# A hybrid decoder layer on one core: where its tiles start within 256 bytes of SBUF

## The chip, the cores and the metric

The kernel runs on one core of one Trainium2 chip. Its time is device microseconds for one launch. Before the change the median of three runs is 795.43 us (793.41 to 795.83).

## The reference

One layer on x of 512 tokens by 1024 features, all in float32:

```python
h = rms_norm(x, norm_mix_w)
z, xbc, dt, q, k, v, f = split(h @ w_in)                  # 1024 x 5664
x = x + concat([ssd(xbc, z, dt), fox(q, k, v, f)]) @ w_out  # 2048 x 1024
h = causal_conv3(rms_norm(x, norm_ffn_w) @ w_up)          # 1024 x 5632
gate, val = split(h)
x = x + (silu(gate) * val) @ w_down                       # 2816 x 1024
```

`ssd` is a chunked state-space mixer with 16 heads, `fox` is causal attention with 16 heads and a forget gate.

## The kernel before

**Products in three parts.** Every large product is made by `mm3` (line 101). A float32 operand A is split into a high part `ah` (rounded to the fp32r format) and a low part `al` = A - `ah`, and three matmuls are added into one PSUM bank: `ah*bh`, `ah*bl`, `al*bh`. ScalarE (ACT) rounds the high part with a copy, VectorE (DVE) makes the low part with a subtraction. Each matmul has a stationary operand of 128 columns, which PE loads ahead of it (the instruction LDWEIGHTS, shown as PEld), and a moving operand of 256 or 512 columns that is streamed through. In a matmul's name in the profile, `pw<-wh,xl` means: into the bank `pw`, moving `wh`, stationary `xl`.

**Three stages with different roles.** In the input projections, `feature_tile` (line 241) has weights stationary and the 512 tokens `xh`, `xl` moving; `wide_block` (line 346, banks `pw`) has tokens stationary and weights `wh`, `wl` moving; the output projection (`out_proj`, `out_part`, banks `po`) has the mixers' outputs stationary (`msh`, `msl` of the state-space heads, `mfh`, `mfl` of attention) and weights moving. All of these stream 512 columns. In the **up projection** weights are stationary and half the tokens are moving, so each matmul streams 256 columns. A Strassen-like scheme makes seven products of each of the inner "quads" of weight tiles (`n0` to `n6`, lines 906 to 969), each product of 24 matmuls; the first of the 11 quads is made plainly, as eight products of 24 (`plain`, line 1004). That is 10 x 168 + 192 = 1872 matmuls. Their moving operands are `uh`, `ul` (operands 0 to 3, in the buffers that `xh`, `xl` had), `sh`, `sl` (operands 4 to 6) and `ghl`. In the **down projection** (lines 1089 on) the gated products are stationary and weights move, 512 columns again, in seven products.

**Order.** All engines' programs are laid out ahead of time by a scheduler that works on the order of the code with priorities (`urgent`), and each engine then runs its list in order. The up projection takes 447 to 685 us of the profiled execution. In it a quad's weights arrive by DMA from SyncE's queue (SP), and three times a DMA of GpSimd's queue (POOL) adds another quarter to the same tile `Ta`; after each, ACT and DVE split it again. `gated` (line 982) makes the convolution on ACT and DVE and the gating on POOL.

**Kept products.** Three intermediate sums of a quad (`y0`, `z2`, `y3`) are copied from PSUM to SBUF by ACT (`keep`, line 896), into a ring of 4 buffers of 2 KB, and used once by DVE (lines 929, 965 and 959).

**Where tiles start.** SBUF addresses follow from the tiles' sizes and the order in which they are made. `small` (line 80) rounds small tiles up to `LINE` = 32 floats, 128 bytes. So every tile that PE reads starts either at 0 or at 128 modulo 256 (called its class here). A column slice that PE takes is a multiple of 256 bytes long, so the class of a tile holds for all slices. In the built program:

| tiles | class before | class after |
|---|---|---|
| `xh`, `xl`; `wh`, `wl` in `wp` (three of four pairs) | 128 | 128 |
| `wh`, `wl` in `pa` (every fourth pair) | 0 | 128 |
| `msh`, `msl`, `mfh`, `mfl` | 0 | 128 |
| `ident` (moving operand of the transposes) | 128 | 128 |
| what is transposed (`prob`, `tok`, `xs`, `y`, `xw`), and `qs`, `ks`, `sc`, `xdt`, `v`, `pt` | 0 | 128 |
| `uh`, `ul`, `sh`, `sl` (moving, up projection) | 128 | 64 |
| `ghl` (moving, 48 matmuls of the first quad) | 0 | 128 |
| the down projection's `oh`, `ol`, `oxh`, `oxl` | 128 | 128 |

"Offset" below is the class of a matmul's moving operand less the class of the stationary operand that PE loads for the next matmul while this one streams.

Of the kernel before, what the change touches and what calls it, by code (L numbers as in the profile page):

```python
# [8 lines left out]
F32 = mybir.dt.float32  # L9
F32R = mybir.dt.float32r  # L10
# [5 lines left out]
P = 128  # L16
SEQ = 512
D = 1024
NK = D // P
# [11 lines left out]
NFF = D_FF // P  # L31

AHEAD = 2000
LINE = 32
WARM = 8
C_SCW, C_SCB, C_FCW, C_FCB, C_QW, C_KW, C_END = 0, 48, 60, 192, 236, 237, 238

# [2 lines left out]
def tile_hybrid_layer(  # L40
# [23 lines left out]
    cp = ctx.enter_context(tc.tile_pool(name="cp", bufs=1))  # L64
# [15 lines left out]
    def small(pool_, shape, tag, bufs=1):  # L80

        n = 1
        for d in shape:
            n *= d
        t = pool_.tile([P, -(-n // LINE) * LINE], F32, tag=tag, name=tag, bufs=bufs)[:, 0:n]
        return t if len(shape) == 1 else t.rearrange("p (a b) -> p a b", b=shape[-1])
# [33 lines left out]
        pool.tensor_tensor(out=dst, in0=dst, in1=mhalf[:, 0 : shape], op=ALU.pow)  # L120

    pc = small(cp, (C_END,), "pc")
    misc = cp.tile([P, 2 * LINE], F32, tag="misc", name="misc")
    taken_columns = [0]

    def columns(n):
# [24 lines left out]
    pxt = ctx.enter_context(tc.tile_pool(name="pxt", bufs=1))  # L151
    actx = ExitStack()
    pa = actx.enter_context(tc.tile_pool(name="pa", bufs=1))
    xh = pxt.tile([P, NK, SEQ], F32R, tag="xh", name="xh")
    xl = pxt.tile([P, NK, SEQ], F32R, tag="xl", name="xl")
    R = pa.tile([P, SEQ], F32, tag="R", name="R")
    r = columns(NTB)
    rhalf = columns(NTB)
# [7 lines left out]
    first = [pa.tile([P, 1024], F32R, tag=t, name=t, bufs=1) for t in ("wh", "wl")]  # L166
# [577 lines left out]
    NH = NFF // 2  # L744
    HT = SEQ // 2
# [2 lines left out]

    ptt = ctx.enter_context(tc.tile_pool(name="ptt", bufs=1, side="right", reuse_waits="tile"))

    ptt.tile([P, 24], F32, tag="rest", name="rest", bufs=1)
    pu_ctx = ExitStack()
    pu = pu_ctx.enter_context(tc.tile_pool(name="pu", bufs=1, side="right", reuse_waits="tile"))
    up_banks = {"Z": pz}
# [2 lines left out]
        return up_banks[tag].tile([P, 2, 512], F32, tag=tag, name=name)  # L757


    oh = pxt.tile([P, NK, SEQ], F32R, tag="xh", name="uh").rearrange("p a b -> p (a b)")  # L760
    ol = pxt.tile([P, NK, SEQ], F32R, tag="xl", name="ul").rearrange("p a b -> p (a b)")
    oh, ol = [t.rearrange("p (n k t) -> p n k t", n=4, k=4) for t in (oh, ol)]
    sh, sl = [pu.tile([P, 3, 4, HT], F32R, tag=t, name=t) for t in ("sh", "sl")]

# [108 lines left out]
    def take(on_act, on_dve=None, at=None):  # L873
        taken[made[0] - 1 if at is None else at] = (on_act, on_dve)
# [19 lines left out]
                halfway[0] = ins  # L894

    def keep(src, name, at=None):
        t = pu.tile([P, 2, HT], F32, tag="kept", name=name, bufs=4)
        take(act.copy(t, src), at=at)
        return t

# [13 lines left out]
    def n0(q, where=None):  # L914
        u = quads[q]
        if not hasattr(u, "w"):
            n0_weights(q, where)
        u.G = two_banks("G", "G")
        product(u.w, 0, u.G, H2, True)
        with urgent():  # L920
            u.y0 = keep(u.G[:, :, H2], "y0", u.at)
# [9 lines left out]
    def n2(q):  # L931
        u = quads[q]
        w = split_up(u.ta)
        more(u.ta, B22, q)
        u.Z = two_banks("Z", "Z")
        product(w, 3, u.Z, H1, True)
        with urgent():
            u.z2 = keep(u.Z[:, :, H1], "z2")

    def n3(q):  # L940
        u = quads[q]
        w = split_up(u.ta)
        more(u.ta, B21, q)
        product(w, 4, u.G, H2)
        with urgent():
            u.y3 = keep(u.G[:, :, H2], "y3")
# [205 lines left out]
    pt_ = ctx.enter_context(tc.tile_pool(name="pt", bufs=1, side="right", reuse_waits="tile"))  # L1152
    held_ops = [pt_.tile([P, NH, HT], F32R, tag=t, name=t) for t in ("oh", "ol")]
    T += [pt_.tile([P, 512 * (b - a)], F32, tag="T%d" % a, name="T%d" % a) for a, b in UNITS[2:]]
    def operand(n):
        if n % 3 == 1:
            pair_ = [pxt.tile([P, NK, SEQ], F32R, tag=t, name="o" + t) for t in ("xh", "xl")]
            return tuple(
                t.rearrange("p a b -> p (a b)")[:, 0 : NH * HT].rearrange("p (a b) -> p a b", b=HT) for t in pair_
            )  # L1160
        if n == 2:
            return held_ops
        where = pt_ if n % 3 == 2 else pb
        return [where.tile([P, NH, HT], F32R, tag=t, name=t) for t in ("oh", "ol")]
# [24 lines left out]
    def units_of(n):  # L1189
        quarter, _, tiles, start, adds = PRODUCTS[n]  # L1190
        nxt = PRODUCTS[n + 1][1] if n + 1 < len(PRODUCTS) else None
        if nxt is not None:
            ops.append(operand(n + 1))
# [162 lines left out]
```

## Time and profile before

| | us |
|---|---|
| median of 3 runs | 795.43 |
| the profiled execution: its own time | 795.52 |
| its span, first to last instruction | 793.5 |
| PE busy | 779.5 (98%) |
| DVE busy | 617.6 (78%) |
| ACT busy | 476.7 (60%) |
| POOL busy | 252.3 (32%) |

The profiled execution is 0.09 us from the median, and 2.0 us of it lie outside the span. The granted clock of TensorE is full in it (0.998). A matmul's duration in the profile runs from its start to its modelled end and overlaps its successors: a matmul of 256 columns is shown with 283 ns though the next one starts 120 ns later. Since matmuls run in order, what PE needs for one is read from the distance between the starts of two, called the pitch here.

### The profile page before, as it was taken

How to read it: one execution, taken by the hardware profiler on the slowest of the kernel's cores; microseconds unless marked ns; L12 is line 12 of the kernel's file. 1: busy time of each engine (PE TensorE's matmuls, PEld its weight loads, DVE VectorE, ACT ScalarE, POOL GpSimd, SP SyncE). 2: the span in 40 equal slices, each digit the busy share in tenths (PEclk: the TensorE clock that was granted, in tenths of full speed). 3: DMA queues.
4: the chain of work that ended last, by engine and by line, in shares of the span. 5: the costliest groups of instructions: out<-in, count | busy, mean ns of one | idle time of the engine just before them, and what ended most of it. 6: DMA issues, size and time to landing. Idle time of an engine off the chain costs nothing.

```text
span 793.5 us, 12355 instructions
## 1 busy us (share of the span) xinstructions
PE 779.5 (98%) x4579; PEld 669.9 (84%) x4579; DVE 617.6 (78%) x923; ACT 476.7 (60%) x833; POOL 252.3 (32%) x296
## 2 busy tenths in 40 slices
PE   9999999999999999999999999999999999999996
PEld 7888877878887878887877999999999999888785
DVE  4896987688567576587875885997999998996674
ACT  7656546562479478685663664665656665765561
POOL 0004231443233362233200004444444443553120
PEclk9999999999999999999999999999999999999999
DMA  9514322431254144253222237788788877899992
GB/s 337 192 58 164 106 90 85 147 132 54 80 160 133 49 137 132 70 173 83 90 80 81 86 81 141 174 186 186 161 185 186 186 176 177 224 252 204 243 184 81
DMA packets 35723, 113.95 MB, mean 144 GB/s; under 512 B 4368, under 2 KB 5456, under 8 KB 35664
## 3 DMA queue, kind: packets, MB, share of 16 engines
q1 hardware_dynamic: 24896, 76.46, 28.3%
q0 software_dynamic: 10336, 36.18, 25.3%
q8 instruction: 36, 0.59, 0.3%
q10 hardware_dynamic: 432, 0.52, 0.2%
q14 instruction: 23, 0.19, 0.1%
HBM read 107.29 MB, written 2.20 MB: 138 GB/s over the span
## 4 chain that ended last, share of the span: by engine, by line
PE 67%; DVE 12%; DMA 8%; issue 7%; POOL 3%; ACT 3%; SPq 0%; POOLq 0%; DVEq 0%; ACTq 0%
PE pw L104 22%; PE po L104 11%; DVE wl L870 8%; PE g L104 6%; PE Z L104 6%; PE G L104 6%; DMA Ta<-in_wup_dram 3%; DVE ua L976 2%; PE o L634 2%; PE pT L624 2%; DMA T<-in_wdown_dram 2%; PE Y L104 2%; PE yd L460 2%; DMA Tb<-in_wup_dram 1%; PE j L104 1%
## 5 line engine op out<-in xcount | busy, mean ns | idle before, releaser
L104 PE MATMUL pw<-wh,xh 128*128 128x512 f32 x256 | 102.4, 402 | 0.0
L104 PE MATMUL pw<-wl,xh 128*128 128x512 f32 x256 | 101.8, 398 | 0.0
L104 PE MATMUL pw<-wh,xl 128*128 128x512 f32 x256 | 101.5, 398 | 0.0
L98 DVE TENSOR_TENSOR wl<-wraw,wh 128x1024 fp32r<-128x1024 f32 x59 | 76.0, 1288 | 15.1 <-ACT wh L97 14.7
L97 ACT CAST wh<-wraw 128x1024 fp32r<-128x1024 f32 x59 | 61.8, 1047 | 28.0 <-PE po L104 11.8
L104 PE MATMUL G<-uh,wh 128*128 128x256 f32 x264 | 75.0, 284 | 0.4 <-DVE Z L965 0.4
L104 PE MATMUL G<-uh,wl 128*128 128x256 f32 x264 | 74.7, 284 | 0.2 <-DVE wl L870 0.2
L104 PE MATMUL G<-ul,wh 128*128 128x256 f32 x264 | 74.7, 283 | 0.0
L870 ACT CAST wh<-Ta 128x1024 fp32r<-128x1024 f32 x40 | 41.9, 1048 | 36.5 <-DMA Ta<-in_wup_dram 24.5
L870 DVE TENSOR_TENSOR wl<-Ta,wh 128x1024 fp32r<-128x1024 f32 x40 | 50.2, 1261 | 8.7 <-ACT wh L870 8.7
L104 PEld LDWEIGHTS pw<-wh,xl 128*128 128x128 f32 x256 | 48.2, 188 | 10.0 <-issue 0.5
L104 PEld LDWEIGHTS pw<-wl,xh 128*128 128x128 f32 x256 | 48.2, 188 | 9.7 <-issue 0.7
L104 PEld LDWEIGHTS pw<-wh,xh 128*128 128x128 f32 x256 | 48.1, 188 | 9.6 <-issue 0.5
L870 DVE TENSOR_TENSOR wl<-Tb,wh 128x1024 fp32r<-128x1024 f32 x20 | 50.0, 2500 | 7.5 <-ACT wh L870 7.4
L904 POOL DMA_DIRECT2D Ta<-in_wup_dram x30 | 26.3, 877 | 81.8 <-DVE wl L870 81.5
L104 PEld LDWEIGHTS G<-uh,wh 128*128 128x128 f32 x264 | 50.6, 192 | 0.8 <-DVE Z L965 0.6
L104 PEld LDWEIGHTS G<-uh,wl 128*128 128x128 f32 x264 | 50.5, 192 | 0.5 <-DVE wl L870 0.5
L104 PEld LDWEIGHTS G<-ul,wh 128*128 128x128 f32 x264 | 50.6, 192 | 0.0
L1112 ACT CAST wh<-T 128x1024 fp32r<-128x1024 f32 (+1 forms) x30 | 29.4, 980 | 35.2 <-DMA T<-in_wdown_dram 16.7
L1112 DVE TENSOR_TENSOR wl<-T,wh 128x1024 fp32r<-128x1024 f32 (+1 forms) x30 | 34.0, 1134 | 20.5 <-ACT wh L1112 20.4
L603 DVE CUSTOM_DVE_ANT_0 prob<-S,prob 128x128 f32<-128x128 f32 (+1 forms) x64 | 30.3, 486 | 24.9 <-PE S L602 24.6
L607 ACT ACTIVATE prob<-prob,nm 128x128 f32<-128x128 f32 (+1 forms) x64 | 35.8, 560 | 21.1 <-DVE nm L603 20.8
(294 smaller groups left out, 2436.1 us busy)
## 6 DMA issues: line engine op xcount, KB each, us to landing
Ta<-in_wup_dram POOLq DMA_DIRECT2D x30, 512.0 KB, 5.5
T<-in_wdown_dram POOLq DMA_DIRECT2D x20, 512.0 KB, 7.8
wraw<-in_wqk_dram SPq DMA_DIRECT2D x16, 512.0 KB, 3.6
wraw<-in_wout_dram SPq DMA_DIRECT2D x16, 512.0 KB, 3.3
wraw<-in_wup_dram SPq DMA_DIRECT2D x14, 512.0 KB, 3.4
wraw<-in_wxbc_dram SPq DMA_DIRECT2D x11, 512.0 KB, 6.3
Ta<-in_wup_dram SPq DMA_DIRECT2D x10, 512.0 KB, 5.8
Tb<-in_wup_dram SPq DMA_DIRECT2D x10, 512.0 KB, 5.2
```

What stands on the lines that cost most here:

```text
L97: act.copy(h, r)
L98: dve.tensor_tensor(out=l, in0=r, in1=raw(h), op=ALU.subtract)
L104: ins = pe.matmul(o, a, b, start=start and n == 0, stop=stop and n == 2, **kw)
L460: pe.matmul(yd[:, h * HD : (h + 1) * HD], sc[:, h, :], xdt[:, h * HD : (h + 1) * HD], start=True, stop=True)
L603: dve.tensor_tensor_reduce(out=p, in0=sps[:, :n], in1=p, scale=-1.0, scalar=-NEG, op0=ALU.add, op1=ALU.min, accum_out=nm[:, qb : qb + 1],)
L607: act.activation(p, p, AF.Exp, scale=-1.0, bias=nm[:, qb : qb + 1], accum_out=sm[:, qb : qb + 1])
L624: pe.transpose(t[:, w : w + P], prob[:, o : o + P], ident)
L634: ins = pe.matmul(o[rows, kb * P :], v[:, kb, (2 * pair + i) % 8, :], pt[:, w : w + SEQ - kb * P], start=kb == 0, stop=kb == NTB - 1, skip ...
L870: ordered(act.copy(h, r), lambda: dve.tensor_tensor(out=l, in0=r, in1=raw(h), op=SUB))
L904: last_more[0] = nc.gpsimd.dma_start(t, wup[quarter, q], accum_op=ALU.add)
L976: dve.scalar_tensor_tensor(out=a[:, s:], in0=o[:, : SEQ - s], scalar=pc[:, cw + 2 - s : cw + 3 - s], in1=a[:, s:], op0=ALU.mult, op1=ALU.add,)
L1112: ordered(act.copy(hs, src[:, :n]), lambda: dve.tensor_tensor(out=ls, in0=src[:, :n], in1=raw(hs), op=SUB))
```

## The change

`LINE` becomes 64 floats, so `small` rounds to 256 bytes; `misc` keeps its 64 columns. The two big token tiles in the pool `pxt` are 256 bytes longer, and a helper `moved` gives a view into them that begins at a given float. `xh`, `xl` and the down projection's `oxh`, `oxl` begin at 0; `uh`, `ul` begin at float 48, which is 192 bytes on. A spacer tile ahead of the pool `pu` grows from 24 to 40 floats, so that `sh` and `sl` start 192 bytes past the class of the weights too, and another spacer of 48 floats stands in the pool `pt`. To make room the ring `kept` has 3 buffers in place of 4.

```diff
-LINE = 32
+LINE = 64
...
-    misc = cp.tile([P, 2 * LINE], F32, tag="misc", name="misc")
+    misc = cp.tile([P, LINE], F32, tag="misc", name="misc")
...
-    xh = pxt.tile([P, NK, SEQ], F32R, tag="xh", name="xh")
-    xl = pxt.tile([P, NK, SEQ], F32R, tag="xl", name="xl")
+
+    def moved(tag, name, first=0):
+        return pxt.tile([P, NK * SEQ + LINE], F32R, tag=tag, name=name)[:, first : first + NK * SEQ]
+
+    xh, xl = [moved(t, t).rearrange("p (a b) -> p a b", b=SEQ) for t in ("xh", "xl")]
...
-    ptt.tile([P, 24], F32, tag="rest", name="rest", bufs=1)
+    ptt.tile([P, 24 + LINE // 4], F32, tag="rest", name="rest", bufs=1)
...
-    oh = pxt.tile([P, NK, SEQ], F32R, tag="xh", name="uh").rearrange("p a b -> p (a b)")
-    ol = pxt.tile([P, NK, SEQ], F32R, tag="xl", name="ul").rearrange("p a b -> p (a b)")
+    oh, ol = [moved(t, n, LINE - LINE // 4) for t, n in (("xh", "uh"), ("xl", "ul"))]
...
-        t = pu.tile([P, 2, HT], F32, tag="kept", name=name, bufs=4)
+        t = pu.tile([P, 2, HT], F32, tag="kept", name=name, bufs=3)
...
+    pt_.tile([P, LINE - LINE // 4], F32, tag="rest", name="rest", bufs=1)
     def operand(n):
         if n % 3 == 1:
-            pair_ = [pxt.tile([P, NK, SEQ], F32R, tag=t, name="o" + t) for t in ("xh", "xl")]
-            return tuple(
-                t.rearrange("p a b -> p (a b)")[:, 0 : NH * HT].rearrange("p (a b) -> p a b", b=HT) for t in pair_
-            )
+            return tuple(moved(t, "o" + t)[:, 0 : NH * HT].rearrange("p (a b) -> p a b", b=HT) for t in ("xh", "xl"))
```

The instructions of all five engines stand in the same order before and after, with the same operands and shapes. Beside the addresses only a few waits differ. The one that recurs is in the up projection, on ACT, at the copy of `z2`. Before, around that copy in one quad:

```order
474 L870 CAST wh<-wraw 128x1024 [waits DMAHW4_49,DVE_49,PE_49]
475 L974 ACTIVATE ua<-Z,pc 128x512 [waits DVE_49]
476 L898 COPY z_5460<-Z 128x512 [waits PE_49]
477 L870 CAST wh<-Tb 128x1024 [waits DMAHW6_49,Activation_49]
478 L974 ACTIVATE ua<-Z,pc 128x512 [waits DVE_49,Pool_49]
```

and after:

```order
474 L872 CAST wh<-wraw 128x1024 [waits DMAHW4_49,DVE_49,PE_49]
475 L976 ACTIVATE ua<-Z,pc 128x512 [waits DVE_49]
476 L900 COPY z_5460<-Z 128x512 [waits PE_49,Activation_49]
477 L872 CAST wh<-Tb 128x1024 [waits DMAHW6_49,Activation_49]
478 L976 ACTIVATE ua<-Z,pc 128x512 [waits DVE_49,Pool_49]
```

With three buffers `z2` of a quad takes the place of `y3` of the quad before, so the copy also waits for ACT's own earlier copy there. In the down projection the load of the tile `T4` waits for PE in addition, since it now lies over the end of `sl`, and one gating instruction of POOL waits for a load one instruction or two later than before.

## The prediction

> **What bounds the kernel now.** I read the page's head first, then the granted clock, the groups of PE, and then PE's timeline for the distance between starts.
>
> ```profile
> PE 779.5 (98%) x4579; PEld 669.9 (84%) x4579; DVE 617.6 (78%) x923; ACT 476.7 (60%) x833; POOL 252.3 (32%) x296
> core 0: 793.5 us, clock 0.998
> PE G L104 <- DVE wl L870: 2.7, 8, 1.0
> PE X L104 <- DVE wl L1112: 1.4, 2, 0.8
> ```
>
> PE is busy for 98% of the span at full clock, and its two longest waits in the whole list of waits are 2.7 and 1.4 us. So the pitch of the matmuls sets the time, and the question is whether the pitch depends on where the operands start. The timeline answers for two of the offsets. Columns are start, duration, engine and line; first and last row of a run stand here. Up projection, 256 columns, offset 0 (35 steps between these two rows):
>
> ```profile
> 599.74 0.28 PE L104 MATMUL Z<-uh,wh 128*128 128x256 f32 x1
> ...
> 603.94 0.28 PE L104 MATMUL G<-uh,wl 128*128 128x256 f32 x1
> ```
>
> 4.20 us / 35 = 120.0 ns, and every step between is 0.12: the pitch is locked. The same product with a weight pair of class 0, so offset 128 (21 steps from 471.43 to 473.92, of which the first three and the last are shown):
>
> ```profile
> 471.43 0.27 PE L104 MATMUL G<-ul,wh 128*128 128x256 f32 x1
> 471.54 0.28 PE L104 MATMUL G<-uh,wl 128*128 128x256 f32 x1
> 471.66 0.29 PE L104 MATMUL G<-uh,wh 128*128 128x256 f32 x1
> 471.78 0.28 PE L104 MATMUL G<-ul,wh 128*128 128x256 f32 x1
> ...
> 473.92 0.28 PE L104 MATMUL G<-ul,wh 128*128 128x256 f32 x1
> ```
>
> 2.49 us / 21 = 118.6 ns, and the steps go round between some 0.11 and 0.12. So the start does matter, a little, and offset 128 is not locked. For 512 columns, offset 0 in the down projection (13 steps from 720.05) and offset 128 in an output projection (22 steps):
>
> ```profile
> 720.05 0.39 PE L104 MATMUL Z<-wh,oh 128*128 128x512 f32 x1
> ...
> 723.00 0.39 PE L104 MATMUL Z<-wl,oh 128*128 128x512 f32 x1
> ```
>
> ```profile
> 192.84 0.39 PE L104 MATMUL po<-wl,msh 128*128 128x512 f32 x1
> ...
> 197.95 0.39 PE L104 MATMUL po<-wh,msl 128*128 128x512 f32 x1
> ```
>
> 2.95 / 13 = 226.9 ns against 5.11 / 22 = 232.3 ns: here offset 0 is the better one, by 5.4 ns. But the lock is reached only some way into a run. With transposes in between, offset 0 is no better:
>
> ```profile
> 300.92 1.04 PE L624 MATMUL pT<-ident,prob 128*128 128x128 f32 x8
> L624 PE MATMUL pT<-ident,prob x160: 270/272/328, 236.4 to 423.8; 128*128 128x128 f32 x160
> ...
> 302.02 0.40 PE L104 MATMUL pw<-wh,xh 128*128 128x512 f32 x1
> ...
> 303.41 0.39 PE L104 MATMUL pw<-wh,xh 128*128 128x512 f32 x1
> ```
>
> The six steps from 302.02 to 303.41, all at offset 0, take 231.7 ns each.
>
> **The change part by part.**
>
> (a) *512 columns.* By the table of classes 539 of the 1941 matmuls of 512 columns go from offset 128 to 0. If all lock they gain 539 x 5.4 ns = 2.9 us; if all stay as in the attention stage, 539 x 0.6 = 0.3 us. The longer runs at offset 0 that follow also let neighbours lock that are now disturbed by a change of class. About half the cases lie in projections without transposes, so I take 2.0 us gained, with 0.3 and 2.9 as ends. None of this touches another engine's work, and PE has no cover for it.
>
> (b) *Transposes.* 330 of them have offset 128 now and get 0. The eight in the row above take 1.04 us together; with 0.27 us for the last one (272 ns is the median of 160), the pitch is (1.04 - 0.27)/7 = 110 ns. At offset 0 no row shows transposes. The excess of a locked matmul at offset 0 over an undisturbed one is at most some 10 ns (120 against 110 with half the columns, so this is generous): 0 to 3.3 us lost. I take 0.8 lost, nearer to nothing, because a transpose loads its weights in 140 ns where these products take 192:
>
> ```profile
> L624 PEld LDWEIGHTS pT<-ident,prob 128*128 128x128 f32 x160 | 19.3, 140 | 4.0 <-ACT pt L626 0.4 <-issue 0.2
> L104 PEld LDWEIGHTS G<-uh,wh 128*128 128x128 f32 x264 | 50.6, 192 | 0.8 <-DVE Z L965 0.6
> ```
>
> (c) *The up projection.* 1872 matmuls, of which 1824 go from offset 0 to offset 192 and 48 from 128 to 0. No row of this trace has offset 192. From the nearest rows: the lowest step at offset 128 is 0.11 (471.43 to 471.54), the highest 0.12, the mean 118.6, the lock at offset 0 is 120.0. Offset 192 lies 64 bytes from either measured offset. What these rows show is that the two streams that PE reads at once, moving columns and next weights, get into each other's way at some phases and that the offset sets the phase; a phase that costs less exists, since single steps of 112 to 115 ns occur. The lock at offset 0 lies near the upper end of the steps seen. So from an arbitrary new phase I expect a shorter pitch rather than a longer one, and take the middle between the lowest step (112) and the mean at offset 128 (118.6): 115.4 ns. Offered: 1824 x 4.6 ns = 8.4 us. Ends for the price: 112 all through (14.6 us offered) and 124 (4 ns above the lock, thrice as far as the mean at offset 128 lies below it; 7.3 us lost).
>
> How much of 8.4 us comes through? PE takes 168 x 0.120 = 20.16 us a quad, and the chain of waits shows the period:
>
> ```profile
> 512.15 2.89 PE G L104 x22
> 532.74 2.90 PE G L104 x22
> ```
>
> 20.59 us. What comes next after PE is DVE. Busy time by stretch (columns: stretch, its length, busy and count of PE, PEld, DVE, ACT, POOL, then clock and DMA):
>
> ```profile
> 500.00:530.00 30.00, 29.01 (x242) 28.81 (x241) 29.00 (x30) 19.03 (x26) 14.80 (x16) 1.00 0.84 178
> 530.00:560.00 30.00, 29.31 (x242) 28.91 (x241) 24.62 (x27) 18.07 (x26) 14.61 (x16) 1.00 0.71 157
> 560.00:590.00 30.00, 29.82 (x249) 29.62 (x248) 28.63 (x32) 19.83 (x26) 12.72 (x14) 1.00 0.87 199
> 590.00:620.00 30.00, 29.64 (x245) 29.24 (x245) 28.98 (x26) 18.86 (x25) 16.82 (x17) 1.00 0.76 166
> ```
>
> DVE is busy for 82 to 97% of these. A PE that is 3.8% faster leaves DVE no room in the full stretches, and part of DVE's time is itself waiting, as one step shows:
>
> ```profile
> 569.59 4.62 DVE L870 TENSOR_TENSOR wl<-Tb,wh 128x1024 fp32r<-128x1024 f32 x1 [0.24 <-ACT wh L870]
> 568.88 1.61 POOL L990 TENSOR_TENSOR ua<-ua 128x512 f32<-128x512 f32 x1
> 570.16 1.58 POOL L995 TENSOR_TENSOR KK<-ua 128x512 f32<-128x512 f32 x1
> L870 DVE TENSOR_TENSOR wl<-Ta,wh 128x1024 fp32r<-128x1024 f32 x40 | 50.2, 1261 | 8.7 <-ACT wh L870 8.7
> ```
>
> The subtraction that takes 1.26 us on average takes 4.62 while POOL works on its gating. After a faster PE that step is late first, then the split of the next weights, then PE (the 2.7 us of waits above grow). I count 60% of what is offered: 5.0 us. A longer pitch has no cover at all and would come through in full.
>
> (d) *One kept buffer less.* `z2` of a quad now follows `y3` of the quad before in its buffer. ACT copies `z2` after the sum that reads `y3` on DVE (line 959) is long done:
>
> ```profile
> 574.13 0.69 DVE L959 TENSOR_TENSOR Z<-Z,y 128x512 f32<-128x512 f32 x1
> 580.08 0.59 ACT L898 COPY z<-Z 128x512 f32<-128x512 f32 x1 [1.24 <-PE Z L104]
> ```
>
> 574.82 against 580.08 leaves 5.3 us, and the copy waits for PE then. Nothing; were the slack gone, the copy and the split `wh<-Tb` queued behind it on ACT would be late by what is missing, once a quad. The load of `T4` that now waits for PE's last use of `sl` is issued from 700.47 us on, and that use begins at 679.4: nothing. Copies and subtractions whose tiles change class cost nothing either: ACT's rounding takes the same from `Ta`, which starts at 224, as from `wraw`, which starts at 128.
>
> ```profile
> 700.47 1.81 SPq L1097 DMA_DIRECT2D T<-in_wdown_dram  x4
> L104 PEld LDWEIGHTS G<-sl,wh x160: 187/192/192, 483.0 to 679.4; 128*128 128x128 f32 x160
> L97 ACT CAST wh<-wraw 128x1024 fp32r<-128x1024 f32 x59 | 61.8, 1047 | 28.0 <-PE po L104 11.8
> L870 ACT CAST wh<-Ta 128x1024 fp32r<-128x1024 f32 x40 | 41.9, 1048 | 36.5 <-DMA Ta<-in_wup_dram 24.5
> ```
>
> Sum, against the profiled execution's 795.5: 2.0 gained, 0.8 lost, 5.0 gained: **789.3 us**.
>
> At two places a rule speaks about this. By the Trainium skill, SBUF — State Buffer, section "Who interferes with whom", PE never waits on anyone for SBUF, and TensorE: Matmul & The Clock Gate, section "Step-by-step: what each phase is for", says that loading the next weights takes no read bandwidth from the running matmul. By that the change does nothing (a rival below). The trace disagrees: 226.9 against 232.3 ns between two offsets.
> The second page's section "Wait — 56ns, not 53.3ns?" puts the warm distance at N/2.4 + 2.5 ns, an estimate of 109.2 ns for 256 columns; the trace's 120.0 is 10.8 above it. If offset 192 reached that floor and all came through, (c) would be 19.7 us and the time 774.6.
>
> **The rivals.** Times from the same terms.
>
> 1. *Offset 192 locks at 120 as offset 0 does.* For it: the lock is exact over runs of 35 steps. Against: offset 128 does not lock. Then only (a) and (b) remain: 794.3 us.
> 2. *Offset 192 goes round like offset 128*, mean 118.6: 1824 x 1.4 = 2.6 us offered, 60% is 1.5: 792.8 us.
> 3. *A worse phase (the other side).* The two streams meet more often, and the pitch locks above 120. For it: steps above 120 occur at offset 128 (471.66 from 471.54 is 0.12 after a 0.11), and for 512 columns offset 128 is worse than 0, so a shift can cost. At 124 ns: 7.3 us lost in full, 795.5 + 7.3 - 1.2 = 801.6. It makes the kernel slower by over 0.3% from (2.4 + 1.2)/1.824 = 2.0 ns above the lock on.
> 4. *The start doesn't matter, and the differences seen are those of the stages*: 795.5. Against: the run from 471.43 is the same product as its locked neighbours, with another weight pair alone.
> 5. *PE gets much faster and DVE takes over*: pitch 112 offers 14.6 us, but with DVE at 97% in two of four stretches no more than some 60% can come: 8.8, so 785.5. I count it with the forecast.
>
> **How the numbers follow.** Forecast with 5: 0.47; rival 1: 0.14; rival 2: 0.18; rival 3: 0.16; rival 4: 0.05. The forecast's own range is 784 to 792. For 8 in 10 the range must take in rivals 1, 2 and 4 and the near half of 3 at the top, and the larger gain of 5, with more passing than I count, at the bottom: 778 to 800. A measurement of this kernel can tell 0.3%, 2.4 us, from no change: faster is below 793.0, slower above 797.8. Faster: 0.46 of the forecast, 0.11 of rival 2 and 0.04 of rival 1 make 0.61. Slower: 0.14 of rival 3 and 0.01 of rival 1 make 0.15. Same is the rest, 0.24.
>
> **What would show it.** In the up projection's timeline after the change, the pitch: 113 to 118 for the forecast, 120.0 for rival 1, uneven around 118.6 for rival 2, over 122 for rival 3. In the groups of PE, the mean of `G<-uh,wh` falls from 283 ns by as much as the pitch does. The `po` groups should fall towards the down projection's duration of 0.39, for (a). If the pitch falls and the time doesn't follow, PE's waits for `wl` at line 870 must have grown from 2.7 us, and DVE's busy share in the stretches from 500 us on must stand at 97% or more; then my 60% is what was wrong. The transposes' x8 row tells (b). The forecast is wrong if the pitch of the up projection is 120 or more.

## The result and the profile after

The changed kernel takes 791.80 us (median of 6 runs, 789.41 to 792.62) against 795.98 for the kernel before beside it (6 runs, 793.41 to 798.57). The ratio is 0.9942, with a 95% interval of 0.9917 to 0.9966: faster, by 4.2 us. The forecast was 789.3 with a range of 778 to 800. The profiled execution took 790.07 us with a span of 788.3.

The page after, busy time of the engines, and the chain that ended last by engine:

```profile
PE 767.0 (97%) x4579; PEld 660.2 (84%) x4579; DVE 621.8 (79%) x923; ACT 476.9 (60%) x833; POOL 250.8 (32%) x296
PE 66%; DVE 12%; DMA 10%; issue 7%; ACT 3%; POOL 2%; SPq 0%; DVEq 0%; POOLq 0%; ACTq 0%
```

PE is busy for 12.5 us less, but the span is only 5.2 us shorter: PE now waits. The pitch that changed is on PE's timeline (start, duration, engine and line). Up projection, offset 192, 22 steps between these rows:

```profile
599.46 0.28 PE L104 MATMUL G<-uh,wl 128*128 128x256 f32 x1
599.57 0.28 PE L104 MATMUL G<-uh,wh 128*128 128x256 f32 x1
599.69 0.28 PE L104 MATMUL G<-ul,wh 128*128 128x256 f32 x1
...
601.95 0.28 PE L104 MATMUL Z<-sh,wh 128*128 128x256 f32 x1
```

2.49 us / 22 = 113.2 ns, where it was 120.0. Every step is 113 or 114 ns, from `uh`, `ul` as from `sh`, `sl`: it is a lock again, on a shorter step. An output projection of 512 columns, which went from offset 128 to 0:

```profile
192.78 0.39 PE L104 MATMUL po<-wl,msh 128*128 128x512 f32 x1
...
193.93 0.39 PE L104 MATMUL po<-wl,msh 128*128 128x512 f32 x1
194.16 0.39 PE L104 MATMUL po<-wh,msl 128*128 128x512 f32 x1
194.38 0.39 PE L104 MATMUL po<-wh,msh 128*128 128x512 f32 x1
194.61 0.39 PE L104 MATMUL po<-wl,msh 128*128 128x512 f32 x1
```

Five steps of 0.23 up to 193.93, then 0.68 us / 3 = 226.7 ns: the run settles into the lock, where it stayed near 232 before. The transposes, now at offset 0 too (eight in one row, and the group):

```profile
298.90 1.04 PE L627 MATMUL pT<-ident,prob 128*128 128x128 f32 x8
L627 PE MATMUL pT<-ident,prob x160: 270/272/330, 234.7 to 421.1; 128*128 128x128 f32 x160
```

Again 1.04 us for eight, so (1.04 - 0.27)/7 = 110 ns: nothing changed. In the up projection DVE and PE stand so, by stretches (columns: stretch, its length, busy and count of PE, PEld, DVE, ACT, POOL, then clock and DMA), and the waits say what PE waits for (total us, times, longest):

```profile
500.00:530.00 30.00, 27.20 (x235) 26.72 (x234) 28.69 (x27) 18.33 (x26) 16.18 (x16) 1.00 0.81 168
530.00:560.00 30.00, 28.98 (x255) 28.78 (x255) 28.87 (x30) 20.43 (x27) 12.39 (x13) 1.00 0.80 191
560.00:590.00 30.00, 27.52 (x240) 27.13 (x239) 28.95 (x27) 18.27 (x25) 16.74 (x17) 1.00 0.82 174
590.00:620.00 30.00, 28.56 (x248) 28.16 (x248) 24.81 (x30) 19.41 (x26) 12.03 (x14) 1.00 0.75 177
```

```profile
PE G L104 <- DVE wl L872: 9.5, 8, 1.5
```

PE falls from 29.0 to 29.8 us of each 30 to 27.2 to 29.0, and its wait for `wl` grows from 2.7 to 9.5 us. DVE is full for 28.7 to 29.0 us in three of the four. The chain shows one link of it (start, length, what):

```profile
542.73 1.06 ACT wh L872
543.82 4.82 DVE wl L872
548.68 2.78 PE G L104 x22
```

The timelines of DVE and POOL show what runs while that link takes 4.8 us: four of POOL's gating operations. Experiment 5 tests whether they draw it out.

```profile
543.82 4.81 DVE L872 TENSOR_TENSOR wl<-Tb,wh 128x1024 fp32r<-128x1024 f32 x1
```

```profile
543.31 1.61 POOL L992 TENSOR_TENSOR ua<-ua 128x512 f32<-128x512 f32 x1
544.59 1.57 POOL L997 TENSOR_TENSOR KK<-ua 128x512 f32<-128x512 f32 x1
545.83 1.01 POOL L996 TENSOR_TENSOR sum<-ua 128x256 f32<-128x256 f32 x1
546.53 1.01 POOL L999 TENSOR_TENSOR sum<-ua,KK 128x256 f32<-128x256 f32 x1
```

**Where the 5.2 us of span came from.** I cut the span at the first and at the last matmul of the up projection. In that stage I split further: *offered* is the fall of the mean step (steps under 130 ns, `ghl` left out) times 1824, *stalls* is what steps of 130 ns or more between two matmuls of the stage take beyond the median step.

| us | before | after | gain |
|---|---|---|---|
| first matmul of the up projection at | 447.25 | 444.35 | 2.9 |
| up projection, first to last start | 238.2 | 235.3 | 2.9 |
| mean step under 130 ns | 119.88 ns | 113.98 ns | 10.8 offered |
| stalls in it | 7.5 | 15.4 | -7.9 |
| behind it, to the end of the span | 108.0 | 108.6 | -0.6 |

Of 10.8 us offered by the new pitch 7.9 came back as stalls: 27% passed in this pair of profiles.

### The profile page after: what moved, and what is told of

It reads as the page before. It is cut to its first block, busy times and chain, and to the rows that moved or that the text cites. A ratio compares the mean times of both kernels' runs of the same rounds, so it can differ in the third digit from the quotient of the medians.

```text
span 788.3 us, 12364 instructions
## 1 busy us (share of the span) xinstructions
PE 767.0 (97%) x4579; PEld 660.2 (84%) x4579; DVE 621.8 (79%) x923; ACT 476.9 (60%) x833; POOL 250.8 (32%) x296
## 4 chain that ended last, share of the span: by engine, by line
PE 66%; DVE 12%; DMA 10%; issue 7%; ACT 3%; POOL 2%; SPq 0%; DVEq 0%; POOLq 0%; ACTq 0%
PE pw L104 22%; PE po L104 10%; PE g L104 7%; DVE wl L872 7%; PE Z L104 5%; DMA Ta<-in_wup_dram 5%; PE G L104 5%; PE o L637 2%; PE pT L627 2%; DMA T<-in_wdown_dram 2%; DVE ua L978 2%; PE Y L104 2%; PE yd L463 2%; ACT wh L872 2%; DMA Tb<-in_wup_dram 1%
## 5 line engine op out<-in xcount | busy, mean ns | idle before, releaser
L97 ACT CAST wh<-wraw 128x1024 fp32r<-128x1024 f32 x59 | 61.8, 1048 | 28.7 <-PE po L104 11.4
L104 PE MATMUL G<-uh,wl 128*128 128x256 f32 x264 | 73.1, 277 | 1.1 <-DVE wl L872 1.1
L104 PE MATMUL G<-uh,wh 128*128 128x256 f32 x264 | 73.3, 278 | 0.0
L104 PE MATMUL G<-ul,wh 128*128 128x256 f32 x264 | 73.1, 277 | 0.0
L872 ACT CAST wh<-Ta 128x1024 fp32r<-128x1024 f32 x40 | 42.0, 1050 | 37.0 <-DMA Ta<-in_wup_dram 31.9
L872 DVE TENSOR_TENSOR wl<-Tb,wh 128x1024 fp32r<-128x1024 f32 x20 | 51.1, 2556 | 6.4 <-ACT wh L872 6.3
L104 PE MATMUL G<-sh,wl 128*128 128x256 f32 x160 | 45.1, 282 | 8.4 <-DVE wl L872 8.4
```

The lines of the kernel that those rows point to most:

```text
L97: act.copy(h, r)
L104: ins = pe.matmul(o, a, b, start=start and n == 0, stop=stop and n == 2, **kw)
L872: ordered(act.copy(h, r), lambda: dve.tensor_tensor(out=l, in0=r, in1=raw(h), op=SUB))
```

## The experiments

Each ran beside the kernel before on its chip. Single executions of these kernels lie up to some 4 us from their median (the kernel before: 792.63 to 798.90 in 13 runs, median 794.98), so where one execution alone was timed it is read for its trace, not for its time.

**1. Each part alone.** Four kernels on one chip: the classes alone (the up projection back at offset 0), the up projection alone (classes as before), the kept ring alone, and the changed kernel once more. The edits of the first against the changed kernel, of the second and third against the kernel before:

```diff
# classes alone
-    ptt.tile([P, 24 + LINE // 4], F32, tag="rest", name="rest", bufs=1)
+    ptt.tile([P, 24], F32, tag="rest", name="rest", bufs=1)
-    oh, ol = [moved(t, n, LINE - LINE // 4) for t, n in (("xh", "uh"), ("xl", "ul"))]
+    oh, ol = [moved(t, n, 0) for t, n in (("xh", "uh"), ("xl", "ul"))]
-    pt_.tile([P, LINE - LINE // 4], F32, tag="rest", name="rest", bufs=1)
# up projection alone (moved as in the change, tiles 64 floats longer)
-    ptt.tile([P, 24], F32, tag="rest", name="rest", bufs=1)
+    ptt.tile([P, 40], F32, tag="rest", name="rest", bufs=1)
+    oh, ol = [moved(t, n, 48) for t, n in (("xh", "uh"), ("xl", "ul"))]
-        t = pu.tile([P, 2, HT], F32, tag="kept", name=name, bufs=4)
+        t = pu.tile([P, 2, HT], F32, tag="kept", name=name, bufs=3)
+    pt_.tile([P, 48], F32, tag="rest", name="rest", bufs=1)
# kept ring alone
-        t = pu.tile([P, 2, HT], F32, tag="kept", name=name, bufs=4)
+        t = pu.tile([P, 2, HT], F32, tag="kept", name=name, bufs=3)
```

Classes alone:

> The changed kernel with the moving operands of the up projection at offset 0 as well, so every operand of PE is in one class. Theory A (two separate gains: some 2.9 us before the up projection from the 512-column matmuls that go from offset 128 to 0, and some 2.9 us in the up projection from offset 192): the up projection is back at 120.0 ns a matmul and takes as long as before (238.2 us from its first to its last matmul), its first matmul starts some 2.9 us earlier than before, ratio to the kernel before about 0.996. Rival B (all of the gain is the up projection's, and what precedes it differs by chance): ratio 1.000 and the up projection starts at 447 us.

Up projection alone:

> The kernel before with offset 192 for the up projection's moving operands and three kept buffers, everything else in its old class. Theory A: pitch 113.3 ns in the up projection, which takes 235 to 236 us from first to last matmul; nothing gained ahead of it; ratio about 0.996. Rival B: ratio about 0.994, the whole gain. Rival C (the offset alone gives nothing, because DVE bounds the up projection): ratio 1.000 in spite of the pitch.

Kept ring alone:

> The kernel before with three kept buffers in place of four, nothing else. Theory A: the copy of z2 waits for nothing new, ratio 1.000, within 0.2%. Rival D (the shorter ring delays copies on ACT, and hides part of the gain): ratio 1.002 or more, with ACT's waits at the copies grown.

The changed kernel again:

> The changed kernel once more, on the same chip as the three others. Theory A: its gain is the sum of those of the flat kernel and of the up offset alone, ratio 0.993 to 0.995. Rival: the parts don't add, and the ratio is that of one of them.

Measured, with the cuts of the table above from each kernel's profile:

| | median us (runs) | ratio, 95% interval | up starts at | mean step, ns | up lasts | stalls |
|---|---|---|---|---|---|---|
| before | 794.78 (34) | | 447.25 | 119.9 | 238.2 | 7.5 |
| classes alone | 793.84 (12) | 0.9990, 0.9975 to 1.0005 | 443.84 | 120.0 | 239.0 | 8.1 |
| up projection alone | 793.74 (12) | 0.9987, 0.9970 to 1.0005 | 446.33 | 114.7 | 237.5 | 16.3 |
| kept ring alone | 795.60 (12) | 1.0008, 0.9993 to 1.0024 | 446.30 | 119.9 | 237.5 | 6.8 |
| changed kernel | 791.59 (11) | 0.9958, 0.9941 to 0.9975 | 443.89 | 114.6 | 237.4 | 16.5 |

(The row of before has its median from these runs and its cuts from the profile quoted in the prediction.)

The last row's stage holds something else as well. From 614.2 to 617.6 us the granted clock of that profile is 0.5, and 15 steps there take some 213 ns. One stretch of 30 us and one of 1 us:

```profile
590.00:620.00 30.00, 28.27 (x230) 27.86 (x231) 22.97 (x27) 18.64 (x25) 11.93 (x13) 0.94 0.73 169
615.00:616.00 1.00, 1.00 (x6) 1.00 (x6) 1.00 (x3) 0.12 (x1) 1.00 (x2) 0.50 0.00 0
```

The 17 steps that it touches take 1.7 us more than at 113.5 ns. An estimate without it is 235.7 us for the stage, close to the 235.3 of the first profile. The profile of the up projection alone has such a stretch too, at 750.4 to 753.8 us, behind the up projection; the others have none in their stages.

The third buffer costs nothing that can be measured. With the classes alone the lock of the up projection stays at 120.0 ns (35 steps in 4.20 us), and the gain lies ahead of that stage:

```profile
599.75 0.28 PE L104 MATMUL G<-uh,wl 128*128 128x256 f32 x1
...
603.95 0.28 PE L104 MATMUL Z<-sl,wh 128*128 128x256 f32 x1
```

With the up projection alone the step falls to 114.7 ns, and the kernel is hardly faster: PE's wait for `wl` is then 9.8 us (from 2.7), and DVE is busy for 27.7 to 29.3 of each 30 us.

```profile
PE G L104 <- DVE wl L871: 9.8, 9, 1.4
```

```profile
500.00:530.00 30.00, 28.77 (x249) 28.37 (x247) 29.32 (x28) 17.98 (x25) 15.47 (x16) 1.00 0.85 176
590.00:620.00 30.00, 28.46 (x247) 28.06 (x246) 29.25 (x27) 18.56 (x25) 15.71 (x17) 1.00 0.75 165
```

So neither part alone can be told from no change, and both together are 0.42% faster. The two single effects add to 0.23%, which the intervals allow. What does not fit well is the classes alone: in its profile the up projection starts 3.4 us earlier, as in the changed kernel, yet the timed median gains 0.9 us. In that profile the up projection itself is 0.8 us longer than before (239.0 for 238.2).

**2. Other offsets for the up projection.** Only the first float of `uh`, `ul` and the spacers that place `sh`, `sl` change against the changed kernel; the one with 64 and 32 reads:

```diff
-    ptt.tile([P, 24 + LINE // 4], F32, tag="rest", name="rest", bufs=1)
+    ptt.tile([P, 16], F32, tag="rest", name="rest", bufs=1)
-    oh, ol = [moved(t, n, LINE - LINE // 4) for t, n in (("xh", "uh"), ("xl", "ul"))]
+    oh, ol = [moved(t, n, 16) for t, n in (("xh", "uh"), ("xl", "ul"))]
-    pt_.tile([P, LINE - LINE // 4], F32, tag="rest", name="rest", bufs=1)
+    pt_.tile([P, 8], F32, tag="rest", name="rest", bufs=1)
```

`uh`, `ul` at 64 and `sh`, `sl` at 32:

> The changed kernel with uh, ul at offset 64 and sh, sl at offset 32 from the weights. Theory A (the offset sets the phase of two streams, and each offset has its own lock or round): each has a pitch of its own, between 109 and 127 ns, and that of offset 64 isn't that of 192. Rival E (any offset but 0 and 128 gives 113.3): both show 113.3.

At 128 and 96:

> The changed kernel with uh, ul at offset 128 and sh, sl at offset 96. Theory A: offset 128 goes round at a mean of 118.6 ns as it did in the 1 of 11 products before; offset 96 has a pitch of its own. Rival E: offset 96 shows 113.3.

At 224 and 160:

> The changed kernel with uh, ul at offset 224 and sh, sl at offset 160. Theory A: pitches of their own; if the price changes smoothly with the offset, 160 lies between 118.6 (128) and 113.3 (192), and 224 between 113.3 and 120.0. Rival E: both 113.3.

The timeline of the first of them, `uh` and `ul` (11 steps), then `sh` and `sl` (15 steps):

```profile
599.81 0.28 PE L104 MATMUL G<-uh,wh 128*128 128x256 f32 x1
...
601.10 0.28 PE L104 MATMUL G<-uh,wl 128*128 128x256 f32 x1
601.22 0.28 PE L104 MATMUL Z<-sh,wh 128*128 128x256 f32 x1
...
602.97 0.28 PE L104 MATMUL Z<-sh,wh 128*128 128x256 f32 x1
```

117.3 and 116.7 ns here; over the whole stage the means of steps under 130 ns are, by offset (0 from the kernel before, 192 from the profile after):

| offset, bytes | 0 | 32 | 64 | 96 | 128 | 160 | 192 | 224 |
|---|---|---|---|---|---|---|---|---|
| 256 columns, mean step in ns | 119.9 | 117.6 | 116.2 | 119.8 | 118.8 | 117.9 | 114.0 | 118.3 |
| steps seen | one | go round | go round | go round | go round | go round | one | go round |

The locked steps themselves are 120.0 at 0 and 113.3 at 192. In the other profiles at 192 the mean is 114.1 to 114.8, so of the eight, 192 is the best by 1.4 to 2.2 ns, and it and 0 alone lock. The three executions were 788.5, 789.8 and 795.1 us, which can't rank them. Their traces show that the length of the stage does not follow the mean step: it lasts 235.2, 236.7 and 239.2 us at 116.8, 119.2 and 118.1 ns over both operands, and 235.3 to 238.2 us in the five profiles at offset 192 with all of the convolution and the gating on POOL (the result, experiments 1 and 3).

**3. The same shift for 512 columns.** If 192 were simply a good offset, the input projections would gain from it too. Their tokens are moved by 64 bytes, so that the token products with tokens moving get offset 64 and those with weights moving (`pw`) get 192:

```diff
-    xh, xl = [moved(t, t).rearrange("p (a b) -> p a b", b=SEQ) for t in ("xh", "xl")]
+    xh, xl = [moved(t, t, 16).rearrange("p (a b) -> p a b", b=SEQ) for t in ("xh", "xl")]
```

> The changed kernel with the tokens xh, xl of the input projections moved by 64 bytes, so that products with tokens moving (feature tiles, 288 matmuls) have offset 64 and those with weights moving (768 matmuls of the bank pw) offset 192. Theory A: with 512 columns too the offset sets the pitch; if 192 helps as it does with 256 columns, by 6.7 ns, the pw products fall from 226.7 to 220 where they lock, and the kernel gains up to 768 x 6.7 ns = 5.1 us more. Rival F (with 512 columns offset 0 is the best there is): the pitch rises to some 231 ns, and the kernel is 3 to 5 us slower than the changed one.

794.87 us (10 runs), ratio 1.0003 (0.9981 to 1.0026): the whole gain of the change is gone. The up projection starts at 448.1 instead of 444.4. At offset 192 ten steps of `pw` take 2.33 us:

```profile
134.21 0.39 PE L104 MATMUL pw<-wl,xh 128*128 128x512 f32 x1
...
136.54 0.39 PE L104 MATMUL pw<-wh,xl 128*128 128x512 f32 x1
```

233.0 ns, against 226.7 in the lock at 0. In these products the moving weights lie where they lay, and only the stationary tokens are moved: so it is not the start of the moving operand alone that counts. In the up projection the moving operand was moved and the weights stayed. A second kernel then gave several stages of 512 columns other offsets at once (input projections 32 and 224, down projection 160, 64, 96 and 240):

```diff
-    xh, xl = [moved(t, t).rearrange("p (a b) -> p a b", b=SEQ) for t in ("xh", "xl")]
+    xh, xl = [moved(t, t, 8).rearrange("p (a b) -> p a b", b=SEQ) for t in ("xh", "xl")]
+    pb.tile([P, 24], F32, tag="rest", name="rest", bufs=1)
-    pt_.tile([P, LINE - LINE // 4], F32, tag="rest", name="rest", bufs=1)
+    pt_.tile([P, LINE], F32, tag="rest", name="rest", bufs=1)
-            return tuple(moved(t, "o" + t)[:, 0 : NH * HT].rearrange(...) for t in ("xh", "xl"))
+            return tuple(moved(t, "o" + t, 40 if n == 1 else 4)[:, 0 : NH * HT].rearrange(...) for t in ("xh", "xl"))
```

> The changed kernel with several offsets for 512 columns at once: tokens of the input projections moved by 32 bytes (feature tiles at offset 32, the bank pw at 224), in the down projection Y at 160, Z at 64, X at 96 in its first product and 240 in its second. Theory A: each offset has its own lock or round, between 216 and 241 ns; those that don't lock lie at some 231. An offset that locks below 226.7 would be worth that difference on up to 1941 matmuls, with PE as the only bound. Rival F (offset 0 is the best there is for 512 columns): all lie at 226.7 or above.

One execution, 797.4 us. The median steps, with 0 and 192 from the kernels above (226.7 is the locked step; at 64 the feature tiles of the first kernel show 231):

| offset, bytes | 0 | 32 | 64 | 96 | 160 | 192 | 224 | 240 |
|---|---|---|---|---|---|---|---|---|
| 512 columns, median step in ns | 226.7 | 234 | 229 | 231 | 234 | 233 | 234 | 233 |

For 512 columns 0 is the best of those tried and the only one that locks. The change has picked the best of the offsets tried for each of the two widths.

**4. Give DVE room: one tap of the convolution left out, before and after.** If DVE holds the gain back, the same shift must pay more once DVE has less to do. Both kernels lose the tap of two tokens back in the causal convolution:

```diff
-        for s in range(1, 3):
+        for s in range(1, 2):
```

> The kernel before with the convolution's second scalar_tensor_tensor (the tap of two tokens back) left out in the up projection, so DVE has 4 x 0.745 = 3.0 us less to do a quad. Theory A (with 120 ns PE bounds the up projection, DVE only just doesn't): little changes, PE's waits there shrink from some 4 us, and the kernel gains 2 to 5 us. Rival G (DVE bounds the up projection already at 120 ns): a gain of 10 us or more.

> The changed kernel with the same tap left out, so the two differ as before and after do. Theory A (at 113.3 ns DVE bounds it, and that is why little of what the pitch offers came through): now most comes through; the up projection takes some 10 us less than in the kernel before with the tap left out, and the whole some 12 us less than that one. Rival H (what is lost goes to the DMA additions of weights, or to PE itself): the difference of the two stays at some 4 us.

Before without the tap: 789.97 us (8 runs), ratio 0.9937 (0.9916 to 0.9958). After without the tap: 784.41 (5 runs), 0.9868 (0.9846 to 0.9891), both against the kernel before. The shift is worth 5.6 us here instead of 3.2 to 4.2 by the medians; the intervals don't separate these. Within the up projection, which takes 232.8 and then 228.3 us, 4.5 of the 9.5 us come through that the mean steps offer (119.9 to 114.7 ns, 1824 times): nearer to rival H than to A. And the tap alone was worth 5.0 us at the old pitch: the stage fell from 238.2 to 232.8 us and its stalls from 7.5 to 2.3, so DVE held the kernel before back already. The stretches of the first, then of the second:

```profile
530.00:560.00 30.00, 30.00 (x253) 30.00 (x252) 23.43 (x23) 20.82 (x27) 12.04 (x13) 1.00 0.78 186
590.00:620.00 30.00, 30.00 (x253) 30.00 (x252) 23.02 (x24) 20.91 (x27) 12.46 (x14) 1.00 0.78 188
```

```profile
530.00:560.00 30.00, 29.80 (x261) 29.61 (x262) 24.11 (x26) 20.77 (x27) 12.65 (x14) 1.00 0.83 192
590.00:620.00 30.00, 29.74 (x262) 29.54 (x262) 23.70 (x26) 19.83 (x26) 12.44 (x14) 1.00 0.86 197
```

At the old pitch PE is busy for all of both stretches, and DVE has 7 us to spare: PE alone bounds, at 168 x 0.120 = 20.16 us a quad. At the new pitch DVE has 6 us to spare, and PE still has gaps: after the first two, quads take 19.2 to 20.7 us where 168 x 0.1133 = 19.04 are needed. DVE's busy time no longer explains that. The chain of waits from 500 us on, by line, of the first and then of the second:

```profile
by line: PE G L104 64.1%; PE Z L104 25.8%; DMA wraw<-in_wdown_dram 3.9%; PE Y L104 2.9%; DVE wl L1112 1.3%; ACT wh L1112 1.1%; DVE ol L993 0.8%; issue 0.2%; ACTq L1112 0.0%
```

```profile
by line: DMA Ta<-in_wup_dram 25.7%; issue 17.9%; PE G L104 8.8%; POOL KK L997 6.6%; POOL ua L992 6.1%; DVE wl L872 5.8%; ACT wh L872 5.0%; DMA wraw<-in_wdown_dram 4.5%; POOL Ta L906 3.3%; POOL sum L999 3.0%; PE Z L104 2.9%; POOL sum L996 2.
```

In this profile it is now the path of the weights: the DMAs that add into `Ta`, and POOL, which issues them behind its gating. ACT waits for these DMAs (the second kernel, up projection):

```profile
ACT wh L872 <- DMA Ta<-in_wup_dram: 32.8, 17, 3.1
ACT wh L872 <- DMA Tb<-in_wup_dram: 12.1, 9, 2.9
```

These waits alone prove little: the changed kernel with the tap has 31.9 and 5.1 us of them, and the kernel before without it, which PE bounds, 24.4 and 8.4. By the chain a second bound lies close behind DVE's own work, and POOL has a part in it; no run takes the DMAs alone away.

**5. The gating on DVE instead of POOL.** In the changed kernel the six products and sums of the gating move from POOL to DVE, one line of each kind shown. DVE gets more to do, but its subtraction of `Tb` no longer runs beside POOL's gating, and POOL has only its DMA issues left of the two.

```diff
-        pool.tensor_tensor(out=g, in0=g, in1=val[0], op=ALU.mult)
+        dve.tensor_tensor(out=g, in0=g, in1=val[0], op=ALU.mult)
...
-        pool.tensor_tensor(out=S3[:, j, :], in0=g1, in1=g2, op=SUB)
+        dve.tensor_tensor(out=S3[:, j, :], in0=g1, in1=g2, op=SUB)
```

> The changed kernel with the gating's six products and sums of each quad on DVE in place of POOL. DVE gets some 2 x 0.69 + 4 x 0.44 = 3.1 us more to do a quad, and the subtractions no longer stand still while POOL works: those of Tb fall from 2.56 us to some 1.25, which gives back 1.3 us twice a quad, and POOL is free to issue the adding DMAs at once. Theory I (the standing still of DVE behind POOL is what keeps the shorter pitch from coming through): DVE's long steps of 4.4 to 4.9 us vanish, PE's waits for wl fall from some 10 us to under 5, and the kernel is 2 to 4 us faster than the changed one, ratio about 0.991. Theory A' (DVE's total is the bound, standing still included): the two cancel but for 0.5 us a quad more work, the kernel is within 0.3% of the changed one or up to 5 us slower.

785.43 us (4 runs, 783.34 to 785.90) against 795.97 (7 runs): ratio 0.9867 (0.9850 to 0.9883). It is some 6 us faster than the changed kernel, more than the 2 to 4 expected, and so the fastest of all that were run on the whole computation. The groups of this kernel (busy us, mean ns of one, idle before):

```profile
L872 DVE TENSOR_TENSOR wl<-Tb,wh 128x1024 fp32r<-128x1024 f32 x20 | 24.3, 1217 | 3.0 <-ACT wh L872 3.0
L992 DVE TENSOR_TENSOR ua<-ua 128x512 f32<-128x512 f32 x11 | 7.5, 681 | 0.0
```

and of the changed kernel:

```profile
L872 DVE TENSOR_TENSOR wl<-Tb,wh 128x1024 fp32r<-128x1024 f32 x20 | 51.1, 2556 | 6.4 <-ACT wh L872 6.3
L992 POOL TENSOR_TENSOR ua<-ua 128x512 f32<-128x512 f32 x11 | 18.2, 1651 | 8.6 <-DVE oxl L1119 4.9 <-DVE wl L1114 3.7
```

The subtraction of `Tb` falls from 2556 to 1217 ns, and a gating product takes 681 ns on DVE where POOL took 1651. The Trainium skill, SBUF — State Buffer, section "Who interferes with whom", says that a DVE instruction with two inputs in SBUF contends with a POOL instruction that reads SBUF; the two means agree. Stretches and waits of this kernel:

```profile
500.00:530.00 30.00, 29.03 (x249) 28.50 (x248) 25.98 (x39) 18.19 (x26) 4.50 (x6) 1.00 0.73 168
530.00:560.00 30.00, 29.53 (x258) 29.16 (x258) 28.03 (x39) 19.82 (x27) 5.37 (x7) 1.00 0.85 199
560.00:590.00 30.00, 29.14 (x250) 28.62 (x249) 26.36 (x39) 18.49 (x26) 4.94 (x6) 1.00 0.75 171
590.00:620.00 30.00, 29.57 (x256) 29.41 (x255) 28.29 (x39) 20.08 (x27) 5.54 (x7) 1.00 0.83 200
```

```profile
PE G L104 <- DVE wl L872: 0.9, 1, 0.9
```

DVE does six more operations a quad and is hardly fuller for it: it is busy for 108.7 of these 120 us, where it was 111.3 in the profile after and 103.7 in experiment 1's profile of the same kernel. PE's wait for `wl` falls from 9.5 to 0.9 us, and PE leads the chain of waits (470 to 670 us):

```profile
by line: PE G L104 33.1%; issue 17.3%; DVE wl L872 10.4%; DMA Ta<-in_wup_dram 9.6%; DVE ua L978 9.4%; PE Z L104 8.6%; DMA Tb<-in_wup_dram 2.9%; ACT wh L872 2.6%; ACT ua L976 1.1%; DVE sum L999 0.6%; DVE sum L1001 0.6%; ACT wh L1114 0.5%; DV
```

The up projection takes 229.5 us at a mean step of 114.4 ns, with 8.9 us of stalls. So POOL's gating had held the changed kernel back by some 6 us; whether through the drawn-out subtractions or through the DMAs that POOL issues behind it, this run doesn't separate. POOL's issues of `Ta` now wait 49.9 us for DVE's sums, and ACT's wait for these DMAs falls from 31.9 to 24.6 us. Nor does it say what part of the 6 us is due to the pitch: the gating on DVE in the kernel before, at the old pitch, wasn't tried. Against the kernel before the stage is 8.7 us shorter. Without any stall that one would have taken 238.2 - 7.5 = 230.7 us at its old pitch, so by these two profiles no more than 1.2 us of the 8.7 needs the new one.

## Why the prediction was right and wrong

The sign was right, and so was the first half of the mechanism: the offset of the moving operand from the stationary one sets the pitch. The second half, how much of a shorter pitch in the up projection becomes time, was wrong. The time missed by 2.5 us against the median (791.8 for 789.3); against the profiled executions the gain was 5.4 us (795.5 to 790.1) where 6.2 was the sum. That it came so near is in part luck: the up projection gave 2 us less than forecast in the profile after and less still in others, while the transposes cost nothing where 0.8 us was set aside for them, and (a) gave about what was forecast.

(a) *512 columns: 2.0 us forecast.* About right. In the three kernels of experiment 1 and the result that have all classes alike, the up projection starts 443.8 to 444.4 us into the span, in the three with the old classes at 446.3 to 447.3: some 2.6 us, within the ends of 0.3 and 2.9, and nearer the upper one. This holds what (b) may have cost, too. A direct measure is the steps of 150 to 260 ns of these matmuls ahead of the up projection, 1266 of them: 291.3 us in all with the old classes (the profiles of the up projection alone and of the ring alone), 289.4 in each of the three profiles with the new, so 1.9 us. The output projection falls most (mean 231.1 to 228.7 ns), the `pw` products from 230.2 to 228.8. The classes alone were 0.9 us faster by their median, with an interval up to 2.0; what of the earlier start is more than the 1.9 us is not settled.

(b) *Transposes: 0.8 us lost forecast.* Nothing: the eight still take 1.04 us, and the mean step between two transposes is 108.9 ns for 109.0.

(c) *The up projection: 8.4 us offered, 60% passed, 5.0 gained.* Both factors were off, in opposite directions. The pitch is better than the middle I took: locked at 113.3, with a mean of 114.0 to 114.7 for 115.4, so 9.4 to 10.8 us were offered. The share that passes was the error. By the cuts 2.9 us came through in the profile after, 27%. In the changed kernel's profile of experiment 1 it is 0.8 us as it stands, and some 2.5 of 9.7 by the estimate without the half clock; with the up projection alone it is 0.7, in the two kernels of experiment 3 1.8 and 0.0. None comes near 60%. The 60% was not worked out from rows, and a view that spoke against it was there. The prediction took it from PE's 98% and its short waits that the pitch sets the time. But the chain of waits of the kernel before, 470 to 670 us, had DVE in the lead:

```profile
by line: DVE wl L870 29.3%; PE G L104 15.3%; issue 12.5%; DMA Ta<-in_wup_dram 10.9%; PE Z L104 10.1%; DVE ua L976 7.1%; DMA Tb<-in_wup_dram 5.7%; ACT wh L870 5.3%; POOL sum L999 1.1%; ACT ua L974 0.7%; DVE Z L959 0.7%; DVE ol L993 0.4%; DVE
```

Experiment 4 confirms it: less work for DVE made the kernel before 5.0 us faster at its old pitch. The prediction named the sign of this case: the pitch falls, the time does not follow, PE's waits for `wl` grow from 2.7 us and DVE stands at 97% or more. The waits grew to 9.5. DVE stood at 96 to 97% in three of four stretches of the profile after, but at 96, 83, 91 and 77% in experiment 1's profile of the same kernel, whose waits for `wl` are 7.5 us all the same. So the busy share is the weaker of the two signs. What takes the time instead is DVE's path through POOL: moving the gating off POOL took the subtraction of `Tb` from 2556 to 1217 ns and 6 us off the kernel (experiment 5). With DVE relieved in both kernels of a pair, 4.5 of 9.5 us pass, 47%, and there the chain ends in the adding DMAs (experiment 4).

(d) *One kept buffer less: nothing.* Right: 1.0008, with an interval of 0.9993 to 1.0024.

*The rivals.* Rival 1 (a lock at 120) and rival 3 (a worse phase) fell with the first row of the timeline. Rival 2's time, 792.8, is nearer to the measured one than the forecast's, but its reason is wrong: the pitch doesn't go round. Rival 4, that the start doesn't matter, is excluded for both widths by the two tables of offsets, and within one stage by the output projection's steps before and after. Rival 5 comes closest in kind (DVE takes over), but set the share that passes at the same 60%.

## What to carry to other kernels

Where PE is full, measure the distance from start to start of its matmuls, by the offset (modulo 256 bytes) of the moving operand from the stationary operand that is loaded next (within a run both neighbours start in one class here, so the runs don't tell the next one from the matmul's own): here 192 was the best tried for 256 columns and 0 for 512, and a shift that helps one width hurts the other. Before a gain on PE is counted, look at the chain of waits of the stage itself, and not only at busy shares: PE was busy for 98% and DVE still led the chain. An instruction that is drawn out by another engine counts as busy, and a faster PE doesn't shorten it. Work moved from POOL to a nearly full DVE need not make DVE much fuller, when DVE's long instructions ran beside POOL's. And read the granted clock of each stretch before two profiles of one kernel are compared.

## What was not expected of the hardware

The pitches lock on 120.0 ns (offset 0, 256 columns), 113.3 ns (192, 256 columns) and 226.7 ns (0, 512 columns). These are 18, 17 and 34 steps of 6.67 ns. That invites a picture of two streams that take turns on a fixed beat, but only the pitches are shown, here and in the rows from which the prediction drew that two streams get into each other's way; why 192 bytes and 256 columns fit, and why 128 bytes do not, stays open. Offsets that aren't multiples of 32 were tried in one case only (240 with 512 columns, 233 ns).

The lock is an attractor, not a property of single matmuls: after a disturbance a run at offset 0 with 512 columns takes a few matmuls near 230 ns before it is back at 226.7, as the five steps of 0.23 us ahead of 193.93 in the result show. Short runs between transposes gain less from the right offset than long ones: in the output projection of the attention heads, with transposes in between, the mean step fell from 231.2 to 229.4 ns, in that of the state-space heads from 231.0 to 228.0.

Two of the profiles have a single stretch of 3.41 us at half the granted clock amid full clock (experiment 1). What brings it on isn't shown.
